# Latent attention: the values of four heads made in one product 512 columns wide, and a pair's values applied after the next pair's scores

## The chip, the cores and the metric

The kernel runs on one core of one Trainium2 chip. The metric is the device time of one execution in microseconds (us), here the median of three runs. TensorE is called PE below (PEld is its weight load), VectorE DVE, ScalarE ACT, SyncE SP.

## What is computed

One inference step over two layers for 320 tokens (256 of a prompt, 64 of a sample with 128 cached positions). The first layer is multi-head latent attention, the second a stick-breaking attention; each ends in a gated output projection. Only the first layer's attention is changed:

```python
q = (cq @ w_q_up).reshape(B, T, 16, 128 + 64)            # rotary part: the last 64
kv = (ckv_all @ w_kv_up).reshape(B, Tk, 16, 128 + 128)   # per head: keys, then values
k = concat([kv[..., :128], broadcast(kr_all)], -1)
v = kv[..., 128:]
s = einsum('bqhd,bkhd->bhqk', q, k) * 192 ** -0.5        # masked by chunks of 64
p = softmax(s)
o = einsum('bhqk,bkhd->bqhd', p, v).reshape(B, T, 2048) * silu(gate)
return o @ w_o
```

Here `cq` and `ckv` are latents of 512 numbers per token, so each product with an up-projection sums over four blocks of 128.

## The kernel before

Tokens lie on the free axis: prompt 256 and sample 64 make T = 320 columns, with the cached 128 KV = 448. A product in full precision is made of three matmuls in fp32r: `hi*hi`, `hi*lo`, `lo*hi`, where `split` and `plain_split` make a number's high part by an ACT copy (L75, L152) and its low part by a DVE subtraction (L76, L153).

The latent attention is a loop over eight pairs of heads (L468). A pair goes through these stages on PE:

- On even pairs alone, the rotary queries of four heads: two products of 320 columns (`gemm_lora`, L127 to L129). DVE turns them into `rt` (L478), and for each pair into `qr` by six short operations (L510, L511). ACT and DVE make `QA` of it (L512, L513).
- The plain queries of the two heads: two products of 320 columns, taken up as `qn` (DVE, L486) and `qh`, `ql`.
- The keys of the two heads: two products of 448 columns. Each is taken up by three operations that follow one another: `kh` (ACT, L152), `kl` (DVE, L153), `kn` (ACT, L501).
- The values of the two heads: four groups of products, 44 matmuls, with the latents as the stationary operand and 256 columns of weights moving (L528 to L534). The groups give `vv`, `vh` and `vl`, `vo`, `vv` again.
- `scores` (L375): eight matmuls for each head (L386 to L393), the first of which reads `kn` of that head, then eight for the sample's part (L404 to L407). The softmax runs on DVE and ACT (L413 to L421).

Two further stages are not run where they are made but put off in a queue, `steps`, of which `tick` takes one entry after each product: `transposes(j)` (the probabilities of head j, L428) and `values(j)` (probabilities times values, L442 to L451, taken up as `og` by DVE, `ah` by ACT, `al` by DVE, L456 to L464). They run between the products of the next pair.

Each engine works through its own list of instructions in order. The lists of DVE and ACT are not the code's order: a scheduler interleaves the stages when the program is built, and the list is then fixed. PSUM tiles come from pools: three banks `g` for products, two `sc`, two `o`, one `tr`.

Of the kernel before, what the change touches and what calls it, by code (L numbers as in the profile page):

```python
# [18 lines left out]
P = 128  # L19
TP, TS, PAST = 256, 64, 128  # L20
T = TP + TS
# [15 lines left out]
def stream_encoder(  # L37
    ctx: ExitStack,
    tc: tile.TileContext,
    xT, wkv, win, wkr, wmla, wo1, wsb, wo2, ckvp, krp, skp, svp,  # L40
    g0, g1, gf, gq, gkv, cosq, sinq, tabk, qmask, kmask, sbminus, ident, tri,
    y, ockv, okr, ok, ov,
):
# [18 lines left out]
    def tick():  # L62
        if steps:
            for f in steps.popleft():
                f()
# [13 lines left out]
    def load(src, cols=2048):  # L79
        raw = wpool.tile([P, 2048], F32, name="raw")  # L80
        nc.sync.dma_start(raw[:, :cols], src)
        return raw
# [68 lines left out]
    def plain_split(hi, lo, src):  # L151
        s.copy(hi, src)  # L152
        v.tensor_tensor(out=lo, in0=src, in1=f32(hi), op=ALU.subtract)  # L153
# [51 lines left out]
    with ExitStack() as stack:  # L205
# [162 lines left out]
        pq = pb.tile([P, 2 * P], F32, name="pq")  # L368
        v.memset(pq[:, P:], 0.0)

        def mla_pair(pair, qns, QA, QB, ks, vh, vl, vv, vo):

            at = [{}, {}]

# [60 lines left out]

            def values(j):
                h = 2 * pair + j
                vs = slice(j * P, (j + 1) * P)
                if j:
                    at[1]["o"] = pso.tile([P, 512], F32, name="o")  # L440
                o, ph, pl, pt = (at[j][x] for x in ("o", "ph", "pl", "pt"))
                pe.matmul(o[:, 0:TP], vh[:, vs], ph, start=True, stop=False)  # L442
                pe.matmul(o[:, 0:TP], vh[:, vs], pl, start=False, stop=False)
                pe.matmul(o[:, 0:TP], vl[:, vs], ph, start=False, stop=False)
                pe.matmul(o[:, P:TP], vv[:, 0, vs], pt[:, 0:P], start=False, stop=True)
                if j:
                    past = at[0]["pt"]
                    pe.matmul(o[:, TP:384], vo, pt[:, P:], start=True, stop=False)
                    for i in range(2):
                        c = slice(i * TS, (i + 1) * TS)  # L450
                        pe.matmul(  # L451
                            o[:, TP + i * TS : TP + (i + 1) * TS], vv[:, 1, i * P : (i + 1) * P],
                            past[:, P + i * TS : P + (i + 1) * TS], start=False, stop=i == 1,
                        )
                og = pb.tile([P, TP], F32, name="og")
                v.tensor_tensor(out=og, in0=o[:, :TP], in1=sg[:, h, :TP], op=ALU.mult)  # L456
                plain_split(oh[:, h, :TP], ol[:, h, :TP], og)
                if j:
                    og = pb.tile([P, TP], F32, name="og")[:, :P].rearrange("p (j t) -> p j t", j=2)
                    both = slice(h - 1, h + 1)  # L460
                    v.tensor_tensor(
                        out=og, in0=o[:, TP:384].rearrange("p (j t) -> p j t", j=2), in1=sg[:, both, S], op=ALU.mult
                    )
                    plain_split(oh[:, both, S], ol[:, both, S], og)  # L464
# [3 lines left out]
        for pair in range(H // 2):  # L468
            even = pair % 2 == 0
            if even:  # L470
                raw2 = load(wmla[2 * pair + 1])
                whi, wlo = split(raw2[:, 1024:2048], 1024)
                ab = []
                for j in range(2):
                    ps = gemm_lora(whi, wlo, j, cq_h, cq_l, T)
                    for tab in (cosr, sinr):
                        t = pb.tile([P, T], F32, name="rt", bufs=4)
                        v.tensor_tensor(out=t, in0=ps, in1=tab, op=ALU.mult)  # L478
                        ab.append(t)
            raw = load(wmla[2 * pair])  # L480
            whi, wlo = split(raw[:, 0:1024], 1024)
            qns, ks = [], []
            for j in range(2):
                ps = gemm_lora(whi, wlo, j, cq_h, cq_l, T)
                qn = pb.tile([P, T], F32, name="qn", bufs=2)
                v.tensor_tensor(out=qn, in0=ps, in1=rq, op=ALU.mult)  # L486
                qh, ql = qss[j]
                if j == 0:
                    plain_split(qh[:, 0:192], ql[:, 0:192], qn[:, P:T])
                else:  # L490
                    plain_split(qh[:, 0:P], ql[:, 0:P], qn[:, P:TP])
# [12 lines left out]
            QA = pb.tile([P, 2 * T], F32R, name="QA", bufs=2)  # L504
            QB = QBs[pair % 2]
            qr = pb.tile([ROPE, 2 * T], F32, name="qr")
            for i, (c, src) in enumerate(pair_columns()):
                i = 2 * (pair % 2) + min(i, 1)
                rows = slice(32 * i, 32 * i + 32)
                v.tensor_tensor(out=qr[0:32, c], in0=x1c[rows, src], in1=x2s[rows, src], op=ALU.subtract)  # L510
                v.tensor_tensor(out=qr[32:64, c], in0=x1s[rows, src], in1=x2c[rows, src], op=ALU.add)  # L511
            s.copy(QA[0:ROPE, :], qr)  # L512
            v.tensor_tensor(out=QA[ROPE:P, :], in0=qr, in1=f32(QA[0:ROPE, :]), op=ALU.subtract)  # L513
            s.copy(QB[0:ROPE, :], f32(QA[0:ROPE, :]))
            if not even:
                raw2 = load(wmla[2 * pair + 1][:, :1024], 1024)
            whi, wlo = split(raw2[:, 0:1024], 1024)
            vh = pb.tile([P, 256], F32R, name="vh", bufs=2)
            vl = pb.tile([P, 256], F32R, name="vl", bufs=2)
            vv = pb.tile([P, 2, 256], F32, name="vv", bufs=2)  # L520
            vo = pb.tile([P, P], F32, name="vo", bufs=2)
            for i, t0 in ((0, P), (None, 0), (2, None), (1, T)):
                ps = pg.tile([P, 512], F32, name="g")
                out = ps[:, :256]
                for k in range(LT):
                    w = slice(k * 256, (k + 1) * 256)
                    if t0 is None:
                        pe.matmul(out, own[:, k, :], whi[:, w], start=k == 0, stop=False)  # L528
                        pe.matmul(out, own[:, k, :], wlo[:, w], start=False, stop=k == LT - 1)
                    else:  # L530
                        ts = slice(t0, t0 + P)
                        pe.matmul(out, ckv_h[:, k, ts], whi[:, w], start=k == 0, stop=False)  # L532
                        pe.matmul(out, ckv_l[:, k, ts], whi[:, w], start=False, stop=False)  # L533
                        pe.matmul(out, ckv_h[:, k, ts], wlo[:, w], start=False, stop=k == LT - 1)  # L534
                if i is None:
                    plain_split(vh, vl, out)
                elif t0 is None:

                    other = pb.tile([P, P], F32, name="other")
                    for j in range(2):  # L540
                        rows, rest = slice(TS * j, TS * j + TS), slice(TS - TS * j, P - TS * j)
                        s.copy(other[rows, :], out[rest, j * P : (j + 1) * P])
                        v.tensor_tensor(out=vo[rows, :], in0=out[rows, j * P : (j + 1) * P], in1=other[rows, :], op=ALU.add)
                else:
                    s.copy(vv[:, i, :], out)
                tick()
            scores, transposes, values = mla_pair(pair, qns, QA, QB, ks, vh, vl, vv, vo)
            scores()
            t0, t1 = partial(transposes, 0), partial(transposes, 1)
            v0, v1 = partial(values, 0), partial(values, 1)  # L550
            steps.extend(([], [], [t0], [], [t1], [v0], [v1]))
        wo = gemms([wo1[m] for m in range(KT)], oh, ol)
        ready = next(wo)

# [217 lines left out]
def _tiles(w):  # L772

    k, m = w.shape
    return w.reshape(k // P, P, m // P, P).transpose(2, 1, 0, 3).reshape(m // P, P, -1)
# [74 lines left out]
```

## Time and profile before

| | us |
|---|---|
| median of 3 runs | 1089.12 (1089.04 to 1089.21) |
| the profiled execution | 1089.68 |
| its span | 1087.9 |
| PE busy | 1070.1 (98%) |
| DVE busy | 650.1 (60%) |
| ACT busy | 590.7 (54%) |

The span is the time from the first to the last instruction; 1.8 us of the profiled execution lie around it. The latent attention's pairs take the stretch from about 184 us to 349 us of it. Pairs are counted from 0; pair 0 starts its scores at 199.68 us, pair 1 at 219.01, pair 2 at 241.90. Busy times of PE overlap within the engine, so the time that a matmul takes from the engine is read from the distance between starts, not from its duration.

### The profile page before, as it was taken

How to read it: one execution, taken by the hardware profiler on the slowest of the kernel's cores; microseconds unless marked ns; L12 is line 12 of the kernel's file. 1: busy time of each engine (PE TensorE's matmuls, PEld its weight loads, DVE VectorE, ACT ScalarE, POOL GpSimd, SP SyncE). 2: the span in 40 equal slices, each digit the busy share in tenths (PEclk: the TensorE clock that was granted, in tenths of full speed). 3: DMA queues.
4: the chain of work that ended last, by engine and by line, in shares of the span. 5: the costliest groups of instructions: out<-in, count | busy, mean ns of one | idle time of the engine just before them, and what ended most of it. 6: DMA issues, size and time to landing. Idle time of an engine off the chain costs nothing.

```text
span 1087.9 us, 18443 instructions
## 1 busy us (share of the span) xinstructions
PE 1070.1 (98%) x7403; PEld 1061.1 (98%) x7403; DVE 650.1 (60%) x1335; ACT 590.7 (54%) x1272; POOL 10.1 (1%) x22
## 2 busy tenths in 40 slices
PE   8999999999999999999999999999999999999994
PEld 7999999999999999999999999999999999999994
DVE  6886556787886555555556455555555555554454
ACT  7756555767767544445545463545546364554441
POOL 0000000000000000000000000000000000000000
PEclk9999999999999999999999999999999999999998
DMA  8455443321321654544444434444444443534422
GB/s 314 145 187 189 156 147 106 117 98 59 117 73 64 226 169 174 176 155 164 142 160 146 164 138 147 158 141 165 134 156 155 150 166 117 179 117 155 156 78 97
DMA packets 30310, 159.26 MB, mean 146 GB/s; under 512 B 4152, under 2 KB 9856, under 8 KB 13456
## 3 DMA queue, kind: packets, MB, share of 16 engines
q1 hardware_dynamic: 28336, 151.89, 40.7%
q0 software_dynamic: 1456, 5.98, 1.5%
q8 instruction: 58, 0.95, 0.4%
q10 hardware_dynamic: 432, 0.20, 0.1%
q14 instruction: 28, 0.23, 0.1%
HBM read 149.46 MB, written 8.60 MB: 145 GB/s over the span
## 4 chain that ended last, share of the span: by engine, by line
PE 97%; DVE 1%; DMA 1%; SPq 0%; ACT 0%; issue 0%; DVEq 0%
PE g L87 25%; PE g L90 25%; PE g L88 25%; PE g L127 3%; PE g L129 2%; PE g L128 2%; PE g L532 1%; PE g L534 1%; PE g L533 1%; DMA xt<-xT 1%; PE sc L624 1%; PE tr L428 1%; DVE x L738 1%; PE sc L600 1%; PE o L652 1%; PE o L404 0%
## 5 line engine op out<-in xcount | busy, mean ns | idle before, releaser
L75 ACT CAST whi<-raw 128x512 fp32r<-128x512 f32 x536 | 310.8, 617 | 296.7 <-PE g L88 194.6
L76 DVE TENSOR_TENSOR wlo<-raw,whi 128x512 fp32r<-128x512 f32 x536 | 353.4, 686 | 125.8 <-ACT whi L75 119.0
L87 PE MATMUL g<-x2h,whi 128*128 128x320 f32 x1024 | 306.1, 313 | 0.0
L88 PE MATMUL g<-x2l,whi 128*128 128x320 f32 x1024 | 302.2, 309 | 0.0
L87 PE MATMUL g<-ah,whi 128*128 128x320 f32 x832 | 246.4, 310 | 0.0
L88 PE MATMUL g<-al,whi 128*128 128x320 f32 x832 | 245.9, 309 | 0.0
L88 PEld LDWEIGHTS g<-x2l,whi 128*128 128x128 f32 x1024 | 192.5, 188 | 0.0
L87 PEld LDWEIGHTS g<-x2h,whi 128*128 128x128 f32 x1024 | 192.4, 188 | 0.0
L90 PE MATMUL g<-x2h,wlo 128*128 128x320 f32 x1024 | 171.0, 309 | 0.0
L88 PEld LDWEIGHTS g<-al,whi 128*128 128x128 f32 x832 | 156.2, 188 | 0.1
L87 PEld LDWEIGHTS g<-ah,whi 128*128 128x128 f32 x832 | 156.1, 188 | 0.2
L90 PEld LDWEIGHTS g<-x2h,wlo 128*128 128x128 f32 x1024 | 155.5, 188 | 0.0
L90 PE MATMUL g<-ah,wlo 128*128 128x320 f32 x832 | 138.9, 309 | 0.0
L90 PEld LDWEIGHTS g<-ah,wlo 128*128 128x128 f32 x832 | 126.3, 188 | 0.0
L152 ACT CAST ah<-og 128x256 fp32r<-128x256 f32 (+1 forms) x48 | 17.8, 370 | 34.8 <-DVE og L456 14.7
L713 DVE TENSOR_TENSOR g<-g,r 128x320 f32<-128x320 f32 x16 | 7.9, 492 | 42.0 <-PE g L90 42.0
L615 DVE SCALAR_TENSOR_TENSOR a<-sc,a 128x512 f32<-128x512 f32 x16 | 11.1, 692 | 35.4 <-ACT a L614 35.4
L127 PE MATMUL g<-cq_h,whi 128*128 128x320 f32 x96 | 30.1, 313 | 0.0
L725 DVE TENSOR_TENSOR x<-g,x 128x320 f32<-128x320 f32 x16 | 7.9, 492 | 37.1 <-PE g L90 37.1
L129 PE MATMUL g<-cq_h,wlo 128*128 128x320 f32 x96 | 29.7, 309 | 0.0
L128 PE MATMUL g<-cq_l,whi 128*128 128x320 f32 x96 | 29.7, 309 | 0.0
L674 DVE TENSOR_TENSOR kT<-g,r 128x320 f32<-128x320 f32 (+2 forms) x24 | 8.4, 377 | 34.5 <-PE g L90 34.5
(276 smaller groups left out, 1369.2 us busy)
## 6 DMA issues: line engine op xcount, KB each, us to landing
raw<-wsb SPq DMA_DIRECT2D x64, 1024.0 KB, 4.9
raw<-wo SPq DMA_DIRECT2D x32, 1024.0 KB, 4.9
raw<-win SPq DMA_DIRECT2D x20, 1024.0 KB, 4.9
raw<-wmla SPq DMA_DIRECT2D x12, 1024.0 KB, 4.9
raw<-wkv SPq DMA_DIRECT2D x3, 1024.0 KB, 10.3
xt<-xT SPq DMA_DIRECT2D x18, 160.0 KB, 2.6
ok<-kT POOLq DMA_DIRECT2D x8, 320.0 KB, 3.0
ov<-vT POOLq DMA_DIRECT2D x8, 320.0 KB, 2.6
```

The source lines that it names most:

```text
L75: last[0] = s.copy(hi[:, c], raw[:, c])
L76: last[1] = v.tensor_tensor(out=lo[:, c], in0=raw[:, c], in1=f32(hi[:, c]), op=ALU.subtract)
L87: pe.matmul(out, hi[:, w], xh[:, k, :], start=k == 0, stop=False)
L88: pe.matmul(out, hi[:, w], xl[:, k, :], start=False, stop=False)
L90: pe.matmul(out, lo[:, i * P : (i + 1) * P], xh[:, k, :], start=False, stop=k == KT - 1)
L127: pe.matmul(out, hi[:, w], xh[:, k, :n], start=k == 0, stop=False)
L128: pe.matmul(out, hi[:, w], xl[:, k, :n], start=False, stop=False)
L129: pe.matmul(out, lo[:, w], xh[:, k, :n], start=False, stop=k == LT - 1)
L152: s.copy(hi, src)
L428: pe.transpose(tr[:, i * P : (i + 1) * P], src, ident_t)
L532: pe.matmul(out, ckv_h[:, k, ts], whi[:, w], start=k == 0, stop=False)
L615: v.scalar_tensor_tensor(out=sp, in0=sc, scalar=0.0, in1=sp, op0=ALU.max, op1=ALU.add)
```

## The change

The values of two pairs (four heads) are made in one go, in the odd pair, with 512 columns of weights moving in place of 256. So an even pair has no value products; its scores follow its keys. Since the values do not exist yet when the odd pair starts, the `values` steps of the even pair are held in `late` and queued after the odd pair's scores, ahead of that pair's own steps. The even pair's `transposes` still run in the odd pair. The weights are stored anew: the rotary weights (`wrot`, 512 KB for two pairs) and the value weights (`wval`, 1 MB for two pairs) become arrays of their own.

```diff
-        def mla_pair(pair, qns, QA, QB, ks, vh, vl, vv, vo):
+        def mla_pair(pair, qns, QA, QB, ks, vs4):
...
             def values(j):
                 h = 2 * pair + j
-                vs = slice(j * P, (j + 1) * P)
+                vh, vl, vv, vo = vs4
+                vs = slice(h % 4 * P, h % 4 * P + P)
...
             if even:
-                raw2 = load(wmla[2 * pair + 1])
-                whi, wlo = split(raw2[:, 1024:2048], 1024)
+                vs4 = []
+                whi, wlo = split(load(wrot[pair // 2], 1024), 1024)
...
-            raw = load(wmla[2 * pair])
+            raw = load(wmla[pair])
...
             if not even:
-                raw2 = load(wmla[2 * pair + 1][:, :1024], 1024)
-            whi, wlo = split(raw2[:, 0:1024], 1024)
-            vh = pb.tile([P, 256], F32R, name="vh", bufs=2)
...
-            for i, t0 in ((0, P), (None, 0), (2, None), (1, T)):
-                ps = pg.tile([P, 512], F32, name="g")
-                out = ps[:, :256]
...
+                raw = load(wval[pair // 2])
+                ws = [split(raw[:, i : i + 1024], 1024) for i in (0, 1024)]
+                vh = pb.tile([P, 512], F32R, name="vh")
+                vl = pb.tile([P, 512], F32R, name="vl")
+                vv = pb.tile([P, 2, 512], F32, name="vv")
+                vo = pb.tile([P, 2, P], F32, name="vo")
+                vs4.extend((vh, vl, vv, vo))
+                for i, t0 in ((0, P), (None, 0), (2, None), (1, T)):
+                    out = pg.tile([P, 512], F32, name="g")
+                    for k in range(LT):
+                        whi, wlo = (w[:, k % 2 * 512 : k % 2 * 512 + 512] for w in ws[k // 2])
...
             scores()
-            t0, t1 = partial(transposes, 0), partial(transposes, 1)
-            v0, v1 = partial(values, 0), partial(values, 1)
-            steps.extend(([], [], [t0], [], [t1], [v0], [v1]))
+            if even:
+                steps.extend(([], [], *([partial(transposes, j)] for j in range(2))))
+                late = [[partial(values, j)] for j in range(2)]
+            else:
+                steps.extend((*late, *([partial(f, j)] for f in (transposes, values) for j in range(2))))
```

Three places show what the built programs do with it. Below, line numbers of the changed kernel are one higher from `values` on (L443 for L442, L457 for L456, L479 for L478, L487 for L486, L511 and L512 for L510 and L511), and "waits" names the engine whose semaphore an instruction waits for.

PE in pair 2, from the last matmul of the second head's keys on. Before, the step `values(0)` of pair 1 stands there, and then the value products begin; 44 matmuls of them come before the scores:

```order
L129 MATMUL g<-ckv_h,wlo 128x448
L442 MATMUL o<-ph,vh 128x256
L443 MATMUL o<-pl,vh 128x256
L444 MATMUL o<-ph,vl 128x256
L445 MATMUL o<-pt,vv 128x128
L532 MATMUL g<-whi,ckv_h 128x256 [waits DVE_49]
L533 MATMUL g<-whi,ckv_l 128x256
L534 MATMUL g<-wlo,ckv_h 128x256
```

In the changed kernel the step there is `values(1)` of pair 1, and the scores follow it at once:

```order
L129 MATMUL g<-ckv_h,wlo 128x448
L443 MATMUL o<-ph,vh 128x256 [waits Activation_49]
L444 MATMUL o<-pl,vh 128x256 [waits DVE_49]
L445 MATMUL o<-ph,vl 128x256
L446 MATMUL o<-pt,vv 128x128 [waits Activation_49]
L449 MATMUL o<-pt,vo 128x128
L452 MATMUL o<-pt,vv 128x64 x2
L386 MATMUL sc<-kn,qn 128x128 [waits Activation_49]
L392 MATMUL sc<-KA,QA 128x128 [waits DVE_49]
```

The 44 matmuls between the keys and the scores are gone from this place; what is left are the seven of one `values` step (in pair 0, which has no step to take, nothing is left). Eight matmuls later the second head's scores begin, with `kn` of the second head.

DVE in pair 2, around its two `kl` rows (the low parts of the keys of head one and two). Before:

```order
L153 TENSOR_TENSOR kl<-g,kh 128x448
L153 TENSOR_TENSOR pl<-tr,ph 128x256
L76 TENSOR_TENSOR wlo<-raw,whi 128x512
L510 TENSOR_TENSOR qr<-rt 32x320
L511 TENSOR_TENSOR qr<-rt 32x320
L510 TENSOR_TENSOR qr<-rt 32x64
L511 TENSOR_TENSOR qr<-rt 32x64
L76 TENSOR_TENSOR wlo<-raw,whi 128x512
L456 TENSOR_TENSOR og<-o,sg 128x256
L153 TENSOR_TENSOR kl<-g,kh 128x448
L153 TENSOR_TENSOR al<-og,ah 128x256
```

In the changed kernel:

```order
L457 TENSOR_TENSOR og<-o,sg 128x256 [waits PE_49]
L153 TENSOR_TENSOR kl<-g,kh 128x448 [waits Activation_49]
L153 TENSOR_TENSOR al<-og,ah 128x256 [waits Activation_49]
L76 TENSOR_TENSOR wlo<-raw,whi 128x512
L511 TENSOR_TENSOR qr<-rt 32x320
L512 TENSOR_TENSOR qr<-rt 32x320
L511 TENSOR_TENSOR qr<-rt 32x64
L512 TENSOR_TENSOR qr<-rt 32x64
L511 TENSOR_TENSOR qr<-rt 32x256
L153 TENSOR_TENSOR kl<-g,kh 128x448 [waits Activation_49]
```

The second `kl` has one more `qr` and the step's `al` ahead of it and one `wlo` fewer; the `og` of the step stands ahead of it in both. The five `qr` rows make the rotary queries of the next pair, 3. The same five stand ahead of the second `kl` of pair 0 in the changed kernel; before, there were three of them and one more `wlo`.

DVE at the start of pair 2, where the rotary products are taken up. Before:

```order
L478 TENSOR_TENSOR rt<-g,cosr 128x320
L478 TENSOR_TENSOR rt<-g,sinr 128x320
L478 TENSOR_TENSOR rt<-g,cosr 128x320
L478 TENSOR_TENSOR rt<-g,sinr 128x320
L511 TENSOR_TENSOR qr<-rt 32x320
```

In the changed kernel the two `values` steps of pair 0 run there as well:

```order
L479 TENSOR_TENSOR rt<-g,cosr 128x320 [waits PE_49]
L479 TENSOR_TENSOR rt<-g,sinr 128x320
L457 TENSOR_TENSOR og<-o,sg 128x256 [waits PE_49]
L153 TENSOR_TENSOR al<-og,ah 128x256 [waits Activation_49]
L479 TENSOR_TENSOR rt<-g,cosr 128x320 [waits PE_49]
L479 TENSOR_TENSOR rt<-g,sinr 128x320
L512 TENSOR_TENSOR qr<-rt 32x320 [waits DVE_49]
L457 TENSOR_TENSOR og<-o,sg 128x256 [waits PE_49]
```

So each even pair from pair 2 on takes up four `values` steps, where it took up two before, and the odd pairs take up none.

## Rows read from the trace of the kernel before

**Rows 1.** Profile page: busy time of each engine, and the chain by engine.

```profile
PE 1070.1 (98%) x7403; PEld 1061.1 (98%) x7403; DVE 650.1 (60%) x1335; ACT 590.7 (54%) x1272; POOL 10.1 (1%) x22
...
PE 97%; DVE 1%; DMA 1%; SPq 0%; ACT 0%; issue 0%; DVEq 0%
```

**Rows 2.** Windows in the pairs' stretch: us; busy per engine (the second DVE alone), granted clock, DMA.

```profile
184.00:352.00 168.00, 168.00 (x1222) 164.67 (x1222) 133.84 (x331) 117.25 (x338) 0.00 (x0) 1.00 0.27 89
...
225.04:237.81 12.77, 12.43 (x30) 1.00 0.23 83
```

**Rows 3.** Waits of PE's weight loads, 184 to 370: total, times, longest.

```profile
PEld o L442 <- ACT ph L152: 0.2, 1, 0.2
```

**Rows 4.** Timeline of PE, pair 0: start, duration, instruction.

```profile
194.40 0.28 PE L532 MATMUL g<-whi,ckv_h 128*128 128x256 f32 x1
...
199.68 0.39 PE L386 MATMUL sc<-kn,qn 128*128 128x128 f32 x2
...
200.73 0.39 PE L386 MATMUL sc<-kn,qn 128*128 128x128 f32 x2
...
201.78 0.25 PE L404 MATMUL o<-kh,qh 128*128 128x192 f32 x1
...
202.09 0.27 PE L404 MATMUL o<-kh,qh 128*128 128x192 f32 x1
```

**Rows 5.** Timeline of PE, two matmuls of 512 columns in the second layer.

```profile
512.34 0.39 PE L624 MATMUL sc<-sph,triR 128*128 128x512 f32 x1
512.57 0.40 PE L624 MATMUL sc<-spl,triR 128*128 128x512 f32 x1
```

**Rows 6.** Timeline of ACT, pair 0: second kn, end of softmax; in brackets its wait.

```profile
197.57 0.27 ACT L501 COPY kn<-g 128x128 f32<-128x128 f32 x1 [1.06 <-DVE kl L153]
...
208.17 0.39 ACT L418 ACTIVATE pq<-sil,sm 128x128 f32<-128x128 f32 x1
```

**Rows 7.** Timeline of DVE, pair 0: the second kl, and qr behind it.

```profile
196.93 0.62 DVE L153 TENSOR_TENSOR kl<-g,kh 128x448 fp32r<-128x448 f32 x1
...
198.17 0.22 DVE L511 TENSOR_TENSOR qr<-rt 32x64 f32<-32x64 f32 x1
198.40 0.42 DVE L510 TENSOR_TENSOR qr<-rt 32x256 f32<-32x256 f32 x1
```

**Rows 8.** Timeline of PE, pairs 1 and 2: transposes, values, scores, end of keys.

```profile
208.62 0.49 PE L428 MATMUL tr<-ident_t,p 128*128 128x128 f32 x3
...
214.79 0.28 PE L442 MATMUL o<-ph,vh 128*128 128x256 f32 x1
...
215.49 0.28 PE L529 MATMUL g<-wlo,own 128*128 128x256 f32 x1
...
216.33 0.28 PE L442 MATMUL o<-ph,vh 128*128 128x256 f32 x1
...
217.69 0.28 PE L533 MATMUL g<-whi,ckv_l 128*128 128x256 f32 x1
...
219.01 0.39 PE L386 MATMUL sc<-kn,qn 128*128 128x128 f32 x2
...
234.81 0.28 PE L442 MATMUL o<-ph,vh 128*128 128x256 f32 x1
```

**Rows 9.** Timeline of DVE, pairs 1 and 2.

```profile
216.27 0.41 DVE L456 TENSOR_TENSOR og<-o,sg 128x256 f32<-128x256 f32 x1
217.16 0.43 DVE L153 TENSOR_TENSOR al<-og,ah 128x256 fp32r<-128x256 f32 x1 [0.47 <-ACT ah L152]
...
236.86 0.69 DVE L76 TENSOR_TENSOR wlo<-raw,whi 128x512 fp32r<-128x512 f32 x1
237.47 0.42 DVE L456 TENSOR_TENSOR og<-o,sg 128x256 f32<-128x256 f32 x1
237.81 0.62 DVE L153 TENSOR_TENSOR kl<-g,kh 128x448 fp32r<-128x448 f32 x1
238.36 0.43 DVE L153 TENSOR_TENSOR al<-og,ah 128x256 fp32r<-128x256 f32 x1
```

More of the change, by code (lines that the diff above doesn't have):

```diff
@@ L39, in stream_encoder @@
     tc: tile.TileContext,
-    xT, wkv, win, wkr, wmla, wo1, wsb, wo2, ckvp, krp, skp, svp,
+    xT, wkv, win, wkr, wmla, wrot, wval, wo1, wsb, wo2, ckvp, krp, skp, svp,
     g0, g1, gf, gq, gkv, cosq, sinq, tabk, qmask, kmask, sbminus, ident, tri,
@@ L447, in values @@
                     past = at[0]["pt"]
-                    pe.matmul(o[:, TP:384], vo, pt[:, P:], start=True, stop=False)
+                    pe.matmul(o[:, TP:384], vo[:, pair % 2, :], pt[:, P:], start=True, stop=False)
                     for i in range(2):
-                        c = slice(i * TS, (i + 1) * TS)
+                        c = h % 4 - 1 + i
                         pe.matmul(
-                            o[:, TP + i * TS : TP + (i + 1) * TS], vv[:, 1, i * P : (i + 1) * P],
+                            o[:, TP + i * TS : TP + (i + 1) * TS], vv[:, 1, c * P : (c + 1) * P],
                             past[:, P + i * TS : P + (i + 1) * TS], start=False, stop=i == 1,
@@ L515, in stream_encoder @@
             if not even:
-                raw2 = load(wmla[2 * pair + 1][:, :1024], 1024)
-            whi, wlo = split(raw2[:, 0:1024], 1024)
-            vh = pb.tile([P, 256], F32R, name="vh", bufs=2)
-            vl = pb.tile([P, 256], F32R, name="vl", bufs=2)
-            vv = pb.tile([P, 2, 256], F32, name="vv", bufs=2)
-            vo = pb.tile([P, P], F32, name="vo", bufs=2)
-            for i, t0 in ((0, P), (None, 0), (2, None), (1, T)):
-                ps = pg.tile([P, 512], F32, name="g")
-                out = ps[:, :256]
[L525 to L529, printed above, removed]
-                    else:
[L531 to L546, printed above, removed]
@@ L547, in stream_encoder @@
-            scores, transposes, values = mla_pair(pair, qns, QA, QB, ks, vh, vl, vv, vo)
-            scores()
-            t0, t1 = partial(transposes, 0), partial(transposes, 1)
-            v0, v1 = partial(values, 0), partial(values, 1)
-            steps.extend(([], [], [t0], [], [t1], [v0], [v1]))
+                raw = load(wval[pair // 2])
+                ws = [split(raw[:, i : i + 1024], 1024) for i in (0, 1024)]
+                vh = pb.tile([P, 512], F32R, name="vh")
+                vl = pb.tile([P, 512], F32R, name="vl")
@@ new lines, in stream_encoder @@
+                vv = pb.tile([P, 2, 512], F32, name="vv")
[5 more added lines that the diff above has]
+                        whi, wlo = (w[:, k % 2 * 512 : k % 2 * 512 + 512] for w in ws[k // 2])
+                        if t0 is None:
+                            pe.matmul(out, own[:, k, :], whi, start=k == 0, stop=False)
+                            pe.matmul(out, own[:, k, :], wlo, start=False, stop=k == LT - 1)
+                        else:
+                            ts = slice(t0, t0 + P)
+                            pe.matmul(out, ckv_h[:, k, ts], whi, start=k == 0, stop=False)
+                            pe.matmul(out, ckv_l[:, k, ts], whi, start=False, stop=False)
+                            pe.matmul(out, ckv_h[:, k, ts], wlo, start=False, stop=k == LT - 1)
+                    if i is None:
+                        plain_split(vh, vl, out)
+                    elif t0 is None:
+                        other = pb.tile([P, 2, P], F32, name="other")
+                        heads = out.rearrange("p (a b c) -> p a b c", a=2, b=2)
+                        for j in range(2):
+                            rows, rest = slice(TS * j, TS * j + TS), slice(TS - TS * j, P - TS * j)
+                            s.copy(other[rows], heads[rest, :, j, :])
+                            v.tensor_tensor(out=vo[rows], in0=heads[rows, :, j, :], in1=other[rows], op=ALU.add)
+                    else:
+                        s.copy(vv[:, i, :], out)
+                    tick()
@@ L552, in stream_encoder @@
+            scores, transposes, values = mla_pair(pair, qns, QA, QB, ks, vs4)
+            scores()
+            if even:
+                steps.extend(([], [], *([partial(transposes, j)] for j in range(2))))
+                late = [[partial(values, j)] for j in range(2)]
+            else:
+                steps.extend((*late, *([partial(f, j)] for f in (transposes, values) for j in range(2))))
         wo = gemms([wo1[m] for m in range(KT)], oh, ol)
@@ L794 @@
     kvup = a["mla_w_kv_up"][0].reshape(LORA, H, 256)
-    mla = np.zeros((H, P, 2048), np.float32)
+    mla = np.zeros((H // 2, P, 2048), np.float32)
+    rot = np.zeros((H // 4, P, 1024), np.float32)
+    val = np.zeros((H // 4, P, 2048), np.float32)
     for p in range(H // 2):
         h = slice(2 * p, 2 * p + 2)
-        mla[2 * p, :, :1024] = _tiles(qup[:, h, :128].reshape(LORA, 256)).transpose(1, 0, 2).reshape(P, 1024)
-        mla[2 * p, :, 1024:] = _tiles(kvup[:, h, :128].reshape(LORA, 256)).transpose(1, 0, 2).reshape(P, 1024)
-        mla[2 * p + 1, :, :1024] = kvup[:, h, 128:].reshape(LT, P, 256).transpose(1, 0, 2).reshape(P, 1024)
-        if p % 2 == 0:
-            r = qup[:, 2 * p : 2 * p + 4, 128:].reshape(LORA, 4, 2, 32).transpose(0, 2, 1, 3).reshape(LORA, 256)
-            mla[2 * p + 1, :, 1024:] = _tiles(r).transpose(1, 0, 2).reshape(P, 1024)
+        mla[p, :, :1024] = _tiles(qup[:, h, :128].reshape(LORA, 256)).transpose(1, 0, 2).reshape(P, 1024)
+        mla[p, :, 1024:] = _tiles(kvup[:, h, :128].reshape(LORA, 256)).transpose(1, 0, 2).reshape(P, 1024)
+    for p in range(H // 4):
+        h = slice(4 * p, 4 * p + 4)
+        r = qup[:, h, 128:].reshape(LORA, 4, 2, 32).transpose(0, 2, 1, 3).reshape(LORA, 256)
+        rot[p] = _tiles(r).transpose(1, 0, 2).reshape(P, 1024)
+        val[p] = kvup[:, h, 128:].reshape(LT, P, 512).transpose(1, 0, 2).reshape(P, 2048)
     wsb = _tiles(a["sb_w_in"][0]).reshape(4, H, P, 2048).transpose(1, 0, 2, 3).reshape(4 * H, P, 2048)
@@ L810 @@
         "wmla": mla,
+        "wrot": rot,
+        "wval": val,
         "wo1": _tiles(a["mla_w_o"][0]),
```

## Prediction

> **What bounds the kernel now.** I read the page first: PE is busy for 98% of the span and the chain of work that ended last is 97% PE [rows 1]. The windows say the same of the pairs' stretch: PE is busy through all of it at the full clock (granted 1.00, the level of 2.4 GHz), while DVE is busy for 133.84 of 168 us and ACT for 117.25 [rows 2]. Then the waits: of PE there are none in this stretch, and of its weight loads one of 0.2 us [rows 3]. So here the time is the sum of what the matmuls take, and a change can win in two ways only: fewer or cheaper matmuls, or nothing. It can lose wherever PE comes to wait. DVE is the engine to watch: it has slack over the whole stretch, but in the timeline of pair 2 it is busy for 12.43 of the 12.77 us between the first rotary product's `rt` and the second `kl` [rows 2]. Before, that does no harm, since 5 us of value products stand on PE between the keys and the scores.
>
> **The cheaper value products.** The four groups hold 3 x 12 + 8 = 44 matmuls in each of eight pairs, 352 of 256 columns. In pair 0 the 44 run from 194.40 to 199.68 [rows 4], 0.120 us each, 42.2 us in all. Afterwards 176 of 512 columns remain. The nearest rows are the two 512-column matmuls in the second layer, 0.23 us from start to start [rows 5]: 176 x 0.23 = 40.5. The columns are the same in number; what is saved is the part of each matmul that does not depend on columns, 352 - 176 of them. **Term 1: -1.8 us.**
>
> The Trainium skill ("TensorE: Matmul & The Clock Gate", section "Back-to-back issue gap") gives 131 ns for a matmul of 512 columns in a sustained stream, and ~216 ns for one by itself. By the first figure the 176 would take 23 us (an estimate from that page) and the change would win 19 us. The trace speaks against it: its pair of 512 columns stands 0.23 us apart. I go by the row, and keep the other as a rival.
>
> The weights moved are the same bytes; the splits, four `values` steps' matmuls and the softmax are the same instructions. DVE and ACT take the value groups up in half as many operations of twice the width, in the odd pairs, where 10 us of value products cover them. The loads run ahead of their use by a pair or so, before as after. I cost these at nothing.
>
> **Pair 0: the scores come straight after the keys.** Before, the key products of pair 0 end, and the value products begin, at 194.40 [rows 4]. The second head's `kl` runs on DVE from 196.93 for 0.62 us [rows 7], and `kn`, which waits for it, on ACT from 197.57 to 197.84 [rows 6]: 3.4 us after the keys. The first head's eight score matmuls take 1.05 us (199.68 to 200.73), and in the changed order three of the sample's (0.31, from 201.78 to 202.09) stand with them [rows 4]. Without the value products, the second head's scores could start at 194.40 + 1.36 = 195.76. They need `kn`, at 197.84 as before: DVE's list ahead of the second `kl` loses one `wlo` (0.61, by the step from 236.86 to 237.47 [rows 9]) and gains two of `qr` (0.22 and 0.42 [rows 7]), which is even. **Term 2: +2.1 us**, read almost wholly off rows that the change leaves alone. I see no way for it to be under 1.5.
>
> **Pairs 2, 4 and 6: the same, with DVE later still.** Count from the start of pair 1's scores at 219.01 [rows 8]. Before, pair 2's keys end at 234.81 [rows 8], 15.80 later. The change puts three `values` steps ahead of that point which were not there. A first one costs 0.58 (from 214.79 to 215.49, less one matmul of 0.12), a second one 1.24 (from 216.33 to 217.69, less 0.12) [rows 8]: 15.80 + 0.58 + 1.24 + 0.58 = 18.20. Then another second one, 1.24, and the first head's scores, 1.05: PE is ready for the second head's scores at 20.49.
>
> DVE: before, the second `kl` starts at 237.81 [rows 9], 18.80 after 219.01. To be added ahead of it are:
> - three `al` at 0.35 and two `og` at 0.34, an instruction's duration less the 0.08 by which the next one starts early (237.47, 0.42 and 237.81 [rows 9]): 1.73;
> - the `og` and `al` of the sample part, half as wide, 0.4 together (an estimate from those of 256 columns);
> - one wait: `al` right behind `og` has to wait until ACT has made `ah`. From `og` to `al` is 0.89 in such a place (216.27 to 217.16 [rows 9]), 0.55 more than 0.34;
> - one `qr` of 0.42 [rows 7], less one `wlo` of 0.61.
>
> That is 2.5 us: `kl` from 21.3 to 21.9, `kn` done at 22.2. PE waits 22.2 - 20.49 = 1.7. Three times this: **term 3: +5.1 us.** What hides these operations today are the value products behind the keys; with them gone the whole of the lateness is paid. One wait is contained in it: PE's second late step needs the `o` bank that the first one's `og` reads, and may stand 0.3 us at the start of the pair, which DVE's lateness swallows.
>
> No row shows the new list at work, so the bounds: at least 0 per pair, if DVE absorbs all that is added in gaps (then `kn` is done at 18.80 + 0.62 + 0.29 = 19.7, before 20.49); at most some 3, if both late steps' `al` and the step ahead of `kl` wait 0.55 each. I take 1.7, since DVE's list had only 0.34 us of gaps in this stretch [rows 2] and is fixed when the program is built. Who waits behind the late `kn`: the second head's scores, and then softmax, whose result the next pair's `transposes` need. In pair 1 before, the softmax's last operation ends at 208.56 [rows 6] and the first transposition starts at 208.62 [rows 8]: no slack at all. But a later start of the scores shifts both alike, so I take nothing for it, at most 1 us in each of four odd pairs.
>
> After pair 7 nothing changes: two steps more run before the last transposes, and the projection's products cover them.
>
> **The sum.** -1.8 + 2.1 + 5.1 = +5.4 us, on the profiled execution's 1089.68: 1095.1, with a span of 1093.3. That execution lies 0.56 above the median of the runs, and the sum carried to the median of 1089.12 is **1094.5 us**, 0.5% slower.
>
> **The rivals.**
> - *Partly covered.* DVE finds its added work in gaps: the stalls of pairs 2, 4 and 6 lie between 0 and 0.9 each. Then only pair 0 is sure: from -1.8 + 2.1 = +0.3 to +3, 1089.4 to 1092.1. For it: DVE has 34 us of slack in 168. Against it: the slack lies in the odd pairs.
> - *Not slower: the keys are taken up in time.* If the second `kn` is done before PE asks for it in all pairs, only term 1 is left: 1087.3. The point that decides is `kn` within 2.3 us of the end of the keys (1.4 in pair 0). Against it stands pair 0, where it took 3.4 us with the same list.
> - *Deeper: the odd pairs wait too.* In the even pairs' softmax DVE also has the last step's `og` and `al` and a `QA` to do between the maxima, so the probabilities come late for the transposes: up to 1 us in each of four odd pairs, 1098.5.
> - *512 columns cost far less here than in the second layer*: 19 us faster, 1070. Rows 5 are against it.
>
> **How the numbers follow.** Chances: as forecast (+3 to +8) 0.58; partly covered 0.22; not slower 0.10; deeper 0.08; the cheap 512 columns 0.02. I take the forecast's time. The forecast and the partly covered case hold 0.8 together: 1089.4 to 1097.5, the upper end from a stall of 2.5 in each of three pairs and 0.2 elsewhere; the likeliest case alone is 1092.1 to 1097.5. A measurement of this kernel can tell about 0.2%, 2.2 us, from no change. Slower by more holds the forecast, the deeper case and half of the partly covered one: 0.77. Faster by more needs the last rival or an unseen gain: 0.03. The rest, 0.20, is no change to be told.
>
> **What would show it.** Right: start to start of the 512-column value matmuls 0.23; a gap on PE before the second head's L386 in pairs 0, 2, 4, 6, of about 2.1 and 1.7 us, released by `kn` on ACT and behind it `kl` on DVE; DVE without gaps from `rt` to the second `kl`; the stretch from pair 1's scores to pair 3's about 1.2 us longer than before. Wrong: no such gap, or a `kl` that starts within a microsecond of the key products' end; a pitch far from 0.23; or waits at L428 in the odd pairs, which would make it worse.

## The result, and the profile after

The changed kernel takes 1097.11 us (median of 4 runs, 1096.75 to 1098.39) beside 1089.08 before: a ratio of 1.0076 [1.0064, 1.0088], 8.0 us slower. The profiled execution took 1097.29, with a span of 1095.5 against 1087.9.

On the page of the changed kernel, PE has more busy time than before in spite of 176 fewer matmuls, and DVE, which held 1% of the chain of work that ended last, holds 7% of it [rows 1]:

```profile
PE 1071.4 (98%) x7227; PEld 1051.5 (96%) x7227; DVE 648.0 (59%) x1323; ACT 590.0 (54%) x1252; POOL 10.1 (1%) x22
...
PE 90%; DVE 7%; ACT 2%; DMA 1%; issue 0%; SPq 0%; DVEq 0%
```

The windows over the pairs' stretch, with the same columns as before [rows 2]: PE was busy for all of the 168 us before, and now for 161.43, at the full clock as before.

```profile
184.00:352.00 168.00, 161.43 (x985) 147.51 (x984) 125.71 (x303) 110.75 (x301) 0.00 (x0) 1.00 0.25 85
```

The waits in 184 to 370 say where the rest went. There was one of 0.2 us [rows 3]. There are now 11 in which matmuls stood, in two places, for 6.6 us in all. Seen from the weight loads, which run ahead of the matmuls and stop first, the waits are 10.5 us:

```profile
PE sc L386 <- ACT kn L502: 3.3, 5, 1.5
PE tr L428 <- ACT pt L433: 3.3, 6, 0.8
...
PEld tr L428 <- ACT pt L433: 5.2, 6, 1.0
PEld sc L386 <- ACT kn L502: 4.5, 5, 1.7
PEld o L443 <- DVE og L457: 0.6, 3, 0.2
```

The first place was forecast; the second stood only in a rival, for the odd pairs. In pair 0 PE's timeline shows the end of the keys, then a short wait before the first head's scores and a long one before the second head's, where the value products stood [rows 4]:

```profile
193.97 0.36 PE L129 MATMUL g<-ckv_h,wlo 128*128 128x448 f32 x1
194.60 0.49 PE L386 MATMUL sc<-kn,qn 128*128 128x128 f32 x2 [0.27 <-ACT kn L502]
...
195.95 0.27 PE L404 MATMUL o<-kh,ql 128*128 128x192 f32 x1
197.75 0.49 PE L386 MATMUL sc<-kn,qn 128*128 128x128 f32 x2 [1.53 <-ACT kn L502]
```

DVE in those microseconds has the five `qr` rows ahead of the second `kl` (the last of them shown), with no gap above 0.04 us from one to the next [rows 7]:

```profile
196.33 0.42 DVE L511 TENSOR_TENSOR qr<-rt 32x256 f32<-32x256 f32 x1
196.78 0.62 DVE L153 TENSOR_TENSOR kl<-g,kh 128x448 fp32r<-128x448 f32 x1
```

Pair 2 on PE: the second head's transposes wait for `pt` of the first, and later the second head's scores wait for `kn`:

```profile
229.04 0.49 PE L428 MATMUL tr<-ident_t,p 128*128 128x128 f32 x3
...
231.09 0.31 PE L129 MATMUL g<-cq_h,wlo 128*128 128x320 f32 x1
232.17 0.55 PE L428 MATMUL tr<-ident_t,p 128*128 128x128 f32 x3 [0.77 <-ACT pt L433]
...
239.32 0.44 PE L386 MATMUL sc<-kn,qn 128*128 128x128 f32 x2
...
241.09 0.49 PE L386 MATMUL sc<-kn,qn 128*128 128x128 f32 x2 [0.51 <-ACT kn L502]
```

What ACT does just ahead of these two waits: it makes `pt` and `kn`, and has itself waited for DVE both times.

```profile
231.74 0.37 ACT L433 COPY pt<-tr 128x256 f32<-128x256 f32 x1 [0.72 <-DVE pl L153]
...
240.77 0.27 ACT L502 COPY kn<-g 128x128 f32<-128x128 f32 x1 [1.08 <-DVE kl L153]
```

And DVE, at the start of that chain, and the window (us, busy) from pair 2's first `rt` to its second `kl`, where it was busy for 12.43 of 12.77 us before [rows 2]:

```profile
231.29 0.42 DVE L153 TENSOR_TENSOR pl<-tr,ph 128x256 fp32r<-128x256 f32 x1
...
239.67 0.41 DVE L511 TENSOR_TENSOR qr<-rt 32x256 f32<-32x256 f32 x1
240.11 0.62 DVE L153 TENSOR_TENSOR kl<-g,kh 128x448 fp32r<-128x448 f32 x1
```

```profile
224.65:240.11 15.46, 14.57 (x36) 1.00 0.05 8
```

The wait at the transposes comes of the one `tr` bank. ACT's copy to `pt` is the last to read it, and it stands behind `pl`, which DVE does late. The two transposes of a pair stood two products apart before (`[t0], [], [t1]`: in pair 1 the first head's at 208.62 [rows 8], the second's at 212.92); the change queues them without the empty entry, so they stand one product apart, 229.04 and 232.17 here with the wait. The same wait is in the odd pairs 3, 5 and 7; in pair 3:

```profile
251.79 0.37 PE L129 MATMUL g<-ckv_h,wlo 128*128 128x448 f32 x1
252.47 0.55 PE L428 MATMUL tr<-ident_t,p 128*128 128x128 f32 x3 [0.31 <-ACT pt L433]
```

An idle time in brackets counts from the modelled end of the matmul before. The delay is read from the starts: the three rows' waits put the next matmul 0.93, 0.72 and some 0.5 us later than without them (the usual step is 0.147 behind a matmul of 320 columns and 0.20 behind one of 448, and the first head's scores take 1.05 [rows 4]).

Pair 1 has no such wait. ACT's rows say why: from the softmax's last operation (`pq`) to `pt` it takes 3.86 us in pair 1 and in pair 3 alike, but that operation starts 1.52 us ahead of the first transposes in pair 1 (at 205.41) and only 0.90 ahead of them in pair 3 (at 249.09).

```profile
203.89 0.39 ACT L418 ACTIVATE pq<-sil,sm 128x128 f32<-128x128 f32 x1
...
207.75 0.37 ACT L433 COPY pt<-tr 128x256 f32<-128x256 f32 x1
...
248.19 0.39 ACT L418 ACTIVATE pq<-sil,sm 128x128 f32<-128x128 f32 x1
...
252.05 0.37 ACT L433 COPY pt<-tr 128x256 f32<-128x256 f32 x1
```

Pair 1's scores start at 218.75 and pair 3's at 262.98: 44.23 us for two pairs, where it was 42.21 before (219.01 [rows 8] and 261.22). The other two such stretches are the same: 44.22 and 44.25.

```profile
218.75 0.38 PE L386 MATMUL sc<-kn,qn 128*128 128x128 f32 x2
...
262.98 0.38 PE L386 MATMUL sc<-kn,qn 128*128 128x128 f32 x2
```

The row that ends the stretch in the kernel before:

```profile
261.22 0.39 PE L386 MATMUL sc<-kn,qn 128*128 128x128 f32 x2
```

So the time is lost evenly, 2.02 in each of three stretches; the rest is pair 0's 2.1, less what the cheaper matmuls save.

### The profile page after: what moved, and what is told of

It is laid out like the page before. It is cut to its first block, busy times and chain, and to the rows that moved or that the text cites. A ratio compares the mean times of both kernels' runs of the same rounds, so it can differ in the third digit from the quotient of the medians.

```text
span 1095.5 us, 18043 instructions
## 1 busy us (share of the span) xinstructions
PE 1071.4 (98%) x7227; PEld 1051.5 (96%) x7227; DVE 648.0 (59%) x1323; ACT 590.0 (54%) x1252; POOL 10.1 (1%) x22
## 4 chain that ended last, share of the span: by engine, by line
PE 90%; DVE 7%; ACT 2%; DMA 1%; issue 0%; SPq 0%; DVEq 0%
PE g L88 25%; PE g L87 25%; PE g L90 25%; DVE wlo L76 1%; PE g L127 1%; PE g L129 1%; PE g L128 1%; PE g L536 1%; PE g L534 1%; PE g L535 1%; DVE qr L511 1%; DMA xt<-xT 1%; PE sc L629 1%; DVE qr L512 1%; DVE x L743 1%; PE sc L605 1%
```

## The experiments

Two readings were open. By the first, what PE pays in the even pairs is one lateness, that of DVE's fixed list, met wherever PE next needs DVE: mending one wait opens the next. By the second, each wait is a price of its own (the `kn` for want of cover, the `tr` bank for the nearness of two steps) and comes back when its cause goes. A third, that the loss lies in the matmuls themselves, has little room: in pair 1 the 44 matmuls of 512 columns take 10.11 us, from the first of them (below) to pair 1's scores, 0.230 from start to start, as forecast.

```profile
208.64 0.48 PE L534 MATMUL g<-whi,ckv_h 128*128 128x512 f32 x1
```

Ratios are to the kernel before, run on the same chip. The start of pair 0's scores differs by up to 1.3 us between the profiles of kernels that are alike up to there (198.41 and 199.71 in the last two versions of 512 columns), so beside medians the kernels are compared by the stretch from pair 1's scores to pair 3's ("per two pairs").

**Work put into pair 0's gap.** Nine matmuls of 512 columns that nobody reads, between the keys and the scores of pair 0 (extra work):

```diff
+            if pair == 0:
+                fill = pg.tile([P, 512], F32, name="g")
+                for i in range(9):
+                    pe.matmul(fill, ckv_h[:, 0, 0:P], ckv_h[:, 0:2, 0:256], start=i == 0, stop=i == 8)
```

> Nine matmuls of 512 columns that nobody reads are put between the keys and the scores of pair 0 alone, about 2.1 us of work for PE. Theory (in pair 0 PE stands for 2.1 us until the second head's kn is there): the filler takes the place of the wait, the time stays at that of the changed kernel within 0.3 us (1097.1), and the waits of pair 0's scores are gone from the profile. Rival (the loss is work on PE, or is made up later): 2.1 us more, 1099.2.

Measured: 1097.36 us, 1.0078 [1.0065, 1.0090], with the span of the changed kernel, 1095.5. Some 2.07 us of matmuls (9 x 0.23) cost 0.25 in the median, and most of the wait is gone:

```profile
193.66 2.23 PE L553 MATMUL g<-ckv_h 128*128 128x512 f32 x9
...
197.25 0.49 PE L386 MATMUL sc<-kn,qn 128*128 128x128 f32 x2 [0.32 <-ACT kn L502]
```

From the end of the keys to the second head's scores it is 3.58 us in the changed kernel (194.17 to 197.75) and 3.59 here (193.66 to 197.25), with or without the extra work. The three matmuls of the sample's part that stood in the gap before run behind the scores here, some 0.3 us. So pair 0's 2.1 us were PE waiting for `kn`.

**The second `kl` ahead of the next pair's `qr`.** The edit takes away what makes the second `kl` late in the even pairs:

```diff
-                plain_split(kh, kl, ps)
+                made = plain_split(kh, kl, ps)
...
+            with ExitStack() as behind:
+                if not even:
+                    behind.enter_context(tc.issue_after(past_kl))
...
+            past_kl = made.ins
```

> The changed kernel, but in DVE's list the next pair's qr operations stand behind the even pair's second kl. Theory (PE waits for kn because DVE is late, by 1.9 us through the qr operations): the scores' waits shrink from 1.7 to about 0.5 in pair 0 (one wlo moves ahead of kl instead) and from 0.7 to 0 in pairs 2, 4 and 6, together 3.3 us, 1093.8; the transposes' waits stay. Rival (the chain kh, kl, kn is long by itself, the list does not matter): no change, 1097.1.

Measured: 1096.85 us, 1.0072 [1.0058, 1.0085]: not the gain expected. The waits for `kn` fell from 3.3 to 0.7 us (both that are left stand in pair 0), and those for `pt` rose from 3.3 to 5.4:

```profile
PE tr L428 <- ACT pt L433: 5.4, 7, 0.9
PE sc L386 <- ACT kn L502: 0.7, 2, 0.5
```

The `qr` put off land in the odd pairs, whose second transposes now wait 0.9 in the bracket where it was 0.31, and pair 1's wait too. This is the first reading: the work is still ahead of something that PE needs, only of something else.

**The steps alone, with 256 columns.** The kernel before with the change's order of steps, so that the value products still cover the keys in every pair:

```diff
-            steps.extend(([], [], [t0], [], [t1], [v0], [v1]))
+            if even:
+                steps.extend(([], [], *([partial(transposes, j)] for j in range(2))))
+                late = [[partial(values, j)] for j in range(2)]
+            else:
+                steps.extend((*late, *([partial(f, j)] for f in (transposes, values) for j in range(2))))
```

> The kernel before with the steps of the changed one: values of 256 columns in every pair, but a pair's values steps taken up as in the changed kernel. Theory (what is paid is the missing cover between keys and scores, and two transposes close together): no waits for kn; up to 0.9 us at the second transposes in pairs 2, 4 and 6, so 1089.1 to 1092. Rival (the late steps with their work for DVE are the cost by themselves): 1095 or more.

Measured: 1094.84 us, 1.0053 [1.0041, 1.0066], above the theory's range of 1089.1 to 1092 and 0.2 below where the rival begins. No wait for `kn` is left, and yet PE stands at the transposes:

```profile
PE tr L428 <- ACT pt L433: 3.2, 4, 0.8
...
PEld tr L428 <- ACT pt L433: 5.6, 7, 1.2
```

Per two pairs it takes 43.76 (217.91 to 261.67), 1.55 more than before. So the order of the steps by itself costs nearly three quarters of what the change costs, without one 512-column matmul. Whether that is the late steps' work for DVE (the rival) or the nearness of the transposes, is told apart below, by the kernel with the distances kept.

**A second bank for the transposes.** The changed kernel, with the second head's transposes in a bank of the scores' pool:

```diff
-                tr = pst.tile([P, 512], F32, name="tr")
+                tr = pss.tile([P, 512], F32, name="sc") if j else pst.tile([P, 512], F32, name="tr")
```

> The changed kernel, with the second head's transposes in a bank of their own (one of the pool of the scores). The waits of 0.9 (pairs 2, 4, 6) and 0.5 us (pairs 3, 5, 7) before the second transposes go. Theory (in an even pair DVE sets the end, and PE pays the same lateness at one place or the other): in the even pairs the scores' wait grows from 0.7 to about 1.6, only the odd pairs' 1.5 us are won, 1095.6. Rival (the single bank is a cost by itself): 4.3 us won, 1092.8.

Measured: 1098.13 us, 1.0085 [1.0071, 1.0099]. The waits for `pt` are gone, those for `kn` are longer:

```profile
PE sc L386 <- ACT kn L502: 6.3, 5, 1.5
```

In pair 2 the second head's scores wait 1.50 in place of 0.51. In the even pairs, then, taking the bank away buys nothing: PE comes earlier and waits longer for the same `kn`. What should have come back in the odd pairs shows per two pairs in the first and the last of the three stretches (43.69 and 43.70 against 44.23). The one between them takes 45.27: there and in pair 0 something cost 1.6 us each time that no reading held, a fall of TensorE's clock (last section). Less these 3.2 us the profiled execution of 1098.52 would have taken 1095.3, beside 1095.6 expected.

**An empty entry between the odd pairs' transposes.** The even pair's steps, which run in the odd pair, get the distance that they had before:

```diff
-                steps.extend(([], [], *([partial(transposes, j)] for j in range(2))))
+                steps.extend(([], [], [partial(transposes, 0)], [], [partial(transposes, 1)]))
```

> The changed kernel with one product more between the first and the second head's transposes in the odd pairs (the even pair's steps get an empty entry between them). Theory (the single transposition bank is given back late, and value products can cover that): the waits of 0.5 us in pairs 3, 5 and 7 go and nothing comes in their place, 1.5 us won against the changed kernel, 1095.6. Rival (DVE is late and PE pays it elsewhere): 1097.1 as now.

Measured: 1097.11 us, 1.0070 [1.0058, 1.0083], 1.5 above what was expected. The three odd waits are gone, and three of the six at L428 are left:

```profile
PE sc L386 <- ACT kn L502: 3.3, 5, 1.5
PE tr L428 <- ACT pt L433: 2.3, 3, 0.8
```

Per two pairs it takes 43.77 (219.71 to 263.48), then 43.70 and 43.70: 0.46 to 0.55 less than the changed kernel. The 1.5 us so won are lost again in the profiled execution in pair 0, to the clock: two products of 320 columns behind the wait took 5.07 us in place of 3.53, 1.54 more. So the edit does in the pairs what was expected, and the median alone would have hidden it.

**Both together**, the `kl` first and the empty entry (the diffs of the second and the fifth experiment):

> The changed kernel with both repairs: the next pair's qr behind the second kl on DVE, and an empty entry between the transposes in the odd pairs. Theory (with qr put off, the lateness went to the odd pairs' second transposes, 1 us each; there value products can cover it): only the even pairs' second transposes (0.9 each), 0.7 in pair 0 and some tenths are left, 1092. Rival: the lateness finds a third place, 1095 or more.

Measured: 1092.43 us, 1.0029 [1.0017, 1.0040], as expected. The `qr` put off now have room, and what is left is the even pairs' transposes and pair 0's scores:

```profile
PE tr L428 <- ACT pt L433: 2.3, 3, 0.8
PE sc L386 <- ACT kn L502: 0.7, 2, 0.5
```

Alone, the first edit won 0.3 us in the median and the second nothing (1.5 by the stretches, lost to the clock in its profile); together they won 4.7. Each took away a place at which PE waited, and only with both is there no next place for that lateness in the odd pairs.

**Late values at 256 columns, with the distances kept.** The third kernel with empty entries between the transposes in all pairs:

```diff
-                steps.extend(([], [], *([partial(transposes, j)] for j in range(2))))
-                late = [[partial(values, j)] for j in range(2)]
+                steps.extend(([], [], [t0], [], [t1], [], [], []))
+                late = [[v0], [v1]]
             else:
-                steps.extend((*late, *([partial(f, j)] for f in (transposes, values) for j in range(2))))
+                steps.extend((*late, [t0], [], [t1], [], [v0], [v1]))
```

> The kernel before with values steps taken up behind the next pair's scores, and an empty entry between the two transposes everywhere. Theory (late values steps cost nothing where value products stand behind the keys and the transposes are a product apart): 0.2 us at the second late step in pairs 2, 4 and 6 is left, 1089.7. Rival (the late steps' work for DVE is the cost): 1092 or more, as without the empty entries (1094.8).

Measured: 1089.96 us, 1.0006 [0.9997, 1.0015], as expected. PE's matmuls do not wait anywhere in 184 to 370, and of the weight loads' waits those for the `o` bank are left (0.8 us in all), as in the third kernel. So putting the values off, with its work for DVE, costs 0.7 us, no change to be told; standing nearly side by side costs the transposes most or all of the 4.9 us between this kernel and the third. (The edit also sets the odd pair's own `values` steps two products later. The third kernel's waits were not at those steps but at L428.)

**512 columns, two groups in each pair.** The wide value products, but the first two of the four groups in the even pair and the other two in the odd one, so that each pair keeps some 5 us of cover; the steps spaced as in the kernel just told. The value weights are split in both pairs:

```diff
+            if even:
+                raw_v = load(wval[pair // 2])
...
+            ws = [split(raw_v[:, i : i + 1024], 1024) for i in (0, 1024)]
+            for i, t0 in (((0, P), (None, 0)), ((2, None), (1, T)))[pair % 2]:
...
+                steps.extend(([], [], [t0], [], [t1], []))
+                late = [[v0], [v1]]
             else:
+                steps.extend((*late, [t0], [], [t1], [], [v0], [v1]))
```

> 512 columns, but two of the four groups of values in the even pair and two in the odd one, so that five us of value products stand between keys and scores in every pair, and an empty entry between the transposes; the value weights are split twice for it, four more operations of 512 columns each on ACT and DVE for two pairs. Theory (cover and distance are all that was missing): term 1 alone is left, with 0.2 us in pairs 2, 4 and 6: 1087.9. Rival (DVE's lateness comes back, made worse by the splits): 1090 or more.

Measured: 1088.88 us, 0.9998 [0.9989, 1.0007]: the loss is gone, the gain of the wide matmuls not to be seen. One wait is left, for the `o` bank that the first late step's `og` still reads:

```profile
PE o L443 <- DVE og L457: 0.8, 3, 0.3
```

**The late steps a product further apart**, with 512 columns in halves and, as its counterpart, with 256:

```diff
-                steps.extend((*late, [t0], [], [t1], [], [v0], [v1]))
+                steps.extend((late[0], [], late[1], [t0], [], [t1], [v0], [v1]))
```

> The kernel with two groups of 512 columns in each pair, and the two late values steps of an even pair a product further apart. Theory (every wait found so far has a product that covers it, and only the cheaper matmuls are left): the wait of 0.5 us before the second late step in pairs 2, 4 and 6 goes, 1.4 us less than with the steps next to each other, 1087.5; the stretch from pair 1's scores to pair 3's falls below that of the kernel before, 42.2 us, to 41.8. Rival (the splits done twice keep DVE late): no change, 1088.9.

> The same order of steps with 256 columns in every pair, so that only the width of the value products differs from the run beside it (and the splits done twice there). Theory: all covered, the time of the kernel before, 1089.2, and 1.8 us more than with 512 columns. Rival (512 columns are worth more or less than the distance between starts says): a difference away from 1.8 by 1 us or more.

Measured: with 512 columns 1087.92 us (11 runs), 0.9991 [0.9982, 1.0000]; with 256 columns 1090.18, 1.0012 [1.0003, 1.0020]. The first is 0.4 above what was expected, the second 1.0 above. The new arrays of weights are in this version too, so they are not what the changed kernel loses by. PE's two stretches between pair 1's and pair 3's scores are 41.79 us with 512 columns, 0.42 less than before, as forecast,

```profile
216.60 0.38 PE L386 MATMUL sc<-kn,qn 128*128 128x128 f32 x2
...
258.39 0.38 PE L386 MATMUL sc<-kn,qn 128*128 128x128 f32 x2
```

and 42.58 with 256 (216.66 to 259.24).

The gain does not hold through the layer: the next two stretches with 512 columns take 41.87 and 42.16, 0.35 and 0.05 less than before. In the last of them the transposes wait for the probabilities (`pq`), one matmul for 0.22 us at 334.79. Of the 0.79 between the two kernels 0.45 is the price of the narrow matmuls by the forecast's figures. The rest is a wait of the kernel with 256 columns: the second of pair 2's own `values` steps waits for `pt`, and its matmuls take 1.50 us (237.76 to 239.26) where those of the late step before it take 1.16 (225.49 to 226.65). The version with 512 columns in halves is the best of all the kernels, 1.1 us under the one before, which is at the edge of what the measurement can tell.

## Why the prediction was nearly right, point by point

The direction was right, and PE's waits for late work of DVE are the cause, as forecast; one of the two places was right, and the size was 2.6 us short, 5.4 of 8.0. The result lies at the very upper end of the range, and that end was added up wrongly: -1.8 + 2.1 + 3 x 2.5 + 0.2 is +8.0, which makes 1097.1 and not 1097.5. That it was still met is in part luck, since 1.5 of the missing 2.6 us came from pairs for which the sum held nothing.

- **What bounds the kernel.** Right: PE had no wait to lose, and what the change cost is what PE came to wait.
- **Term 1, cheaper matmuls, -1.8.** Right: 0.230 from start to start against 0.23 forecast. The rival in which 512 columns cost far less is refuted. The Trainium skill ("TensorE: Matmul & The Clock Gate", section "Back-to-back issue gap") has 131 ns for such a matmul in a stream; the trace does not agree, and its other figure there, ~216 ns, is 14 ns under the row.
- **Term 2, pair 0, +2.1.** Right: the two waits put the scores 0.43 and 1.70 us later, 2.1 together, and the first experiment fitted that much work in for 0.25 us.
- **Term 3, pairs 2, 4 and 6, +5.1.** The lateness was forecast nearly to the row. Counted from pair 1's scores, the second `kl` starts at 21.36 (forecast 21.3) and `kn` is done at 22.29 (22.2). PE pays 1.85 in each of these pairs (forecast 1.7), 5.5 in all, but in three places: 0.2 at the `o` bank, 0.93 at the second transposes, 0.72 at the scores. That it is one lateness, the fourth kernel shows: with the bank's wait gone, the wait at the scores grew by about as much. So of the signs named in advance, the gap before the second head's scores was there but 0.72 and not 1.7, and the stretch from pair 1 to pair 3 grew by 2.02 and not by 1.2.
- **The step that failed** is what was costed at nothing: the steps' matmuls as "the same instructions", and the odd pairs, where "I take nothing for it". Pairs 3, 5 and 7 lose 0.5 us each, 1.5 in all, because the new queue has the transposes one product apart and there is one `tr` bank. The distance stood in the diff (`[t0], [], [t1]` against two entries side by side), and the forecast read the moved steps for their length and not for what they share. The price in the even pairs was hidden behind term 3, so it went unseen there too: with full cover the third kernel still lost 5.9 us, 4.9 of which went when the steps were spaced.
- **The sum.** -1.8 + 2.1 + 5.5 + 1.5 = 7.3 of the 7.6 us between the spans. The remaining 0.3 was not taken apart. PE also loses 0.06 to 0.1 in starting again behind a wait (0.55 for 0.49 at the transposes, 0.49 for 0.39 at the scores), and over 11 waits that is more than enough for it.
- **The rivals.** *Not slower* and *partly covered* are refuted by the waits (the 0.72 at the scores alone would have borne the second out; with the other two places it is 1.85). *Deeper* came half true. The odd pairs wait at L428 for the bank and not for the probabilities. But what it named is there: DVE does the last step's two `og` and two `al` around pair 2's maxima (from 240.65 to 243.82), and the softmax's last operation starts 7.10 us after the second head's scores, in pair 0 without such a step 6.14. ACT takes up the transposes behind it, so in pair 3 `pt` comes 0.62 us later, counted from the first transposes, than in pair 1, which goes free. The nearness of the transposes lets this lateness reach PE; with a product between them the fifth kernel covered it.

What stays open: the last 0.3 us of the sum, and when the clock falls behind a wait (last section).

## What to carry to other kernels

When a change moves steps, price their distance as well as their length: two steps that share one buffer need between them the whole chain that gives it back, here `ph`, `pl` and `pt` on two engines. An engine with slack over a stretch but a fixed list has its lateness paid at the first place where the bound engine needs it; closing that place alone only moves the wait, so look for the next one before expecting the gain. Keep some independent work behind every product that another engine has to take up, as the halves in each pair did: only so did the wide matmuls show a gain, 0.42, 0.35 and 0.05 us in the three stretches.

## What the runs showed of the hardware that was not expected

A wait of PE can cost more than its length, since TensorE's clock can fall behind it. In the fourth kernel's profile, with the second transposes in another bank, the windows around pair 0's wait for `kn` (us, PE's busy time with its instructions, the granted clock, DMA share, GB/s) show a granted clock of 0.50, the 1.2 GHz level, in the 2 us after it:

```profile
196.00:198.00 2.00, 0.49 (x3) 0.90 0.71 295
198.00:200.00 2.00, 2.00 (x12) 0.50 0.38 160
200.00:202.00 2.00, 2.00 (x13) 0.75 0.00 0
```

The same profile has waits of 1.50 to 1.51 us before the second head's scores in pairs 2, 4 and 6. Behind pair 4's the clock falls again, and the stretch is 1.6 us longer for it; behind pair 2's and pair 6's it stays at 1.00 (pairs 4 and 6 shown):

```profile
288.00:290.00 2.00, 2.00 (x12) 0.56 0.00 0
...
332.00:334.00 2.00, 2.00 (x18) 1.00 0.33 139
```

The kernel with the empty entry has the same fall a little later, behind its wait of 1.53 us in pair 0, and it cost 1.54 there:

```profile
200.00:202.00 2.00, 2.00 (x10) 0.50 0.00 0
```

The changed kernel's profile has a wait of the same 1.53 us at that place and keeps the full clock behind it:

```profile
196.00:198.00 2.00, 0.47 (x6) 1.00 1.02 324
198.00:200.00 2.00, 2.00 (x18) 1.00 0.45 188
```

So waits of the same length are followed by the fall in some places and not in others, even within one execution; what decides it no run here shows. Whether the changed kernel's highest run, 1098.39 us, had one could not be seen, since it left no profile.
